# Two background jobs for the Strassen operands, and the mixers' weight remainders on VectorE and GpSimd in turn

## The chip, the cores and the metric

The kernel runs on one core of one Trainium2 chip. The metric is the device time of one execution in microseconds (us). The engines work side by side, each through its own queue in program order: TensorE (PE in the profile; PEld is its weight load), VectorE (DVE), ScalarE (ACT), GpSimd (POOL) and SyncE (SP, which starts most of the weight loads). Semaphores hold an instruction until the tile that it needs is written.

## The reference

One sequence of 512 tokens, width 1024, float32, goes through three layers. Each layer adds a mixer and then a SwiGLU FFN to the residual, both behind an RMS norm:

```
h = h + mix(rmsnorm(h))
h = h + (silu(u @ w_gate) * (u @ w_up)) @ w_down        # u = rmsnorm(h), d_ff = 2816
layer 0: mix = HGRN2, a gated linear recurrence, 8 heads of 128, chunks of 64 with decay
layer 1: mix = dilated causal attention, 12 heads in three groups
layer 2: mix = merge of NSA attention (compressed, selected, window) and GLA (4 heads, decay)
```

A final norm stands behind layer 1 and behind layer 2.

## The kernel before, in words

**Products.** Activations lie as eight tiles `x[k]` of 128 features by 512 tokens. A float32 operand is held as two tiles in TensorE's reduced format: a head `hi` (a rounded copy) and a remainder `lo` (the value minus its head). Each product is three matmuls, hi by hi, lo by hi and hi by lo (`mm3`). Nearly every instruction is recorded through one helper (line 250), so the tile names tell the operations apart: `u` is the normed input of a projection or of an FFN's first part, `og` HGRN's gated output, `oan` NSA's output, `obh` and `obl` GLA's, `mr` the merged one, `h` the FFN's hidden tile.

**Weights.** A weight arrives in units of up to 1024 columns in `w_raw` (SP's queue). ScalarE copies the head into a tile `w`, and then a subtraction makes the remainder, `w<-w_raw,w` in the profile. The class `Weights` plans both by a fixed schedule, 0.68 us per tile of columns: the head 8.8 us and the remainder 7.5 us ahead of use. The last argument of `plain` says who makes the remainder: `"v"` VectorE, `"g"` GpSimd, or `"d"`, an accumulating DMA on GpSimd's queue (`w<-in_ffn`), which the first part of each FFN uses. Before, GpSimd makes every second remainder of HGRN's last 8 units and of block 2's last 20; VectorE makes the rest.

**FFN.** Of 22 hidden tiles the first 5 (`FC`) are made by plain products from `u`: `gemm` over 10 tiles, gate and up in turn, whose results VectorE takes from PSUM (`gs<-ps,r_bc`, `h<-ps,sg`). The others go by Strassen's scheme on 256-token halves. Its operands, tiles named `E`, come from `strassen_operands` (line 1580): for each pair of x tiles two scaled copies (`E<-x,vec,r_bc`), four sums (`E<-E`), and for each of four operands a head on ScalarE and a remainder on VectorE (`E<-E,E`, or `E_3110<-E,E_3110` in the order lists). The routine is a generator: wherever it yields, it may be left until the tile that it names is ready. `ffn` starts it as a background job as soon as the norm's factor `r_bc` exists, runs the 10 plain tiles, then calls `drain`, which records whatever is left of the background jobs, and then the Strassen products, whose first chain of matmuls runs over all four pairs.

**The order.** Instructions are recorded in one pass. A planner (`Clock`) keeps an estimated time for every engine from fixed costs per operation (an n-column VectorE operation 0.08 + 0.00104 n us, GpSimd 0.13 + 0.0023 n us). After each tile of a projection `tick` goes through the background jobs and lets the first one that is due by this estimate take one step. So the decay steps of HGRN and GLA, the attention heads and the Strassen operands are laid between the projections' matmuls, and a change in an estimate, or in the number of jobs, moves instructions on all engines.

**Names in the mixers.** In HGRN and GLA the decay steps multiply Q and K (`GQ`, `GK` in GLA) by factors `T` or `GF`, `Sd` are masked scores, `cst,K` is a transpose of K, and `cst,o` sums the squares of a pair of heads' outputs `o` for the norm behind which `og` is made. In NSA `P` are probabilities, `PT` their transposes, `VV` the values, `ks` rotated keys.

Of the kernel before, what the change touches and what calls it, by code (L numbers as in the profile page):

```python
# [17 lines left out]
KD = 8  # L18
FF = 22
# [44 lines left out]
FC = 5  # L64

SHARED = {"hgrn": 8, "blk2": 20}

# [113 lines left out]
class Clock:  # L185
# [3 lines left out]
    def __init__(self, hop):  # L189
        self.hop = hop  # L190
        self.free = {"pe": 0.0, "v": 0.0, "a": 0.0, "g": 0.0}
        self.written, self.read = {}, {}
        self.held = []
# [68 lines left out]
class Weights:  # L262
# [7 lines left out]
    def __init__(self, prog, ctx, aps):  # L270
        tc = prog.tc
        self.nc, self.v, self.a, self.g = tc.nc, prog.v, prog.a, prog.g
        self.pool = ctx.enter_context(tc.tile_pool(name="w", bufs=self.ROOM))
        self.units, self.loads, self.todo, self.live = [], [], [], 0
        now = 0.0
        for sec, segments in weight_plan():
            off = 0
            for kind, body in segments:
                if kind == "c":
                    first = sec.startswith("ffn") and off == 0  # L280
                    units = plan_units(sec, body)
                    for n, (cur, w) in enumerate(units):
                        ap = aps[sec][off:off + 128 * w].rearrange("(p n) -> p n", p=128)
                        off += 128 * w
                        widths = [len(c[2]) for c in cur]
                        shared = n >= len(units) - SHARED.get(sec, 0)
                        self.plain(ap, widths, w, now, "d" if first else "g" if shared and n % 2 else "v")
                        now += w / 128 * self.TILE
                    continue
                order = strassen_order(len(body))  # L290
                groups = []
                for _, pairs, _, _ in body:
                    n = 128 * len(pairs)
                    aps_g = []
                    for w in (2 * n, n, n):
                        aps_g.append(aps[sec][off:off + 128 * w].rearrange("(p n) -> p n", p=128))
                        off += 128 * w
                    groups.append({"n": n, "aps": aps_g, "tiles": {}, "split": {}})
                for i, (g, p) in enumerate(order):
                    groups[g].setdefault("at", {})[p] = now + self.SLOT * i  # L300
                    self.units.append(("s", groups[g], p))
                for grp in groups:
                    self.group(grp, grp is groups[-1])
                now += self.SLOT * len(order)
        self.todo.sort(key=lambda x: x[0])
        self.n_todo = self.n_load = 0
        self.at, self.pos, self.idx, self.now = 0, 0, 0, 0.0
        self.look = 1
# [159 lines left out]
class Program:  # L468
# [1108 lines left out]
        self.residual_gemm(merged, "ffn2")  # L1577


    def strassen_operands(self, gain, X):  # L1580

        v, a = self.v, self.a
        for k in range(0, KD, 2):
            B1, B2, t13, t24 = [self.s2("E", (128, 2, 256)) for _ in range(4)]
            for B, i in ((B1, k), (B2, k + 1)):
                v.scalar_tensor_tensor(
                    B.rearrange("p a n -> p (a n)"), self.x[i], gain[:, i:i + 1], self.r_bc, op0=ALU.mult, op1=ALU.mult)
            yield [B2]
            v.tensor_sub(t13[:, 0], B1[:, 0], B1[:, 1])
            v.tensor_sub(t13[:, 1], B2[:, 1], B1[:, 1])  # L1590
            ops, Y = [], {}
            for src, names in ((B1[:, 0:1], ("a1",)), (B2, ("c", "b2")), (t13, ("b1", "a3")), (t24, ("a2", "a4"))):
                if src is t13:
                    yield [t13]
                    v.scalar_tensor_tensor(t24[:, 0], t13[:, 0], -1.0, B2[:, 1], op0=ALU.mult, op1=ALU.subtract)
                    v.scalar_tensor_tensor(t24[:, 1], t24[:, 0], -1.0, B2[:, 0], op0=ALU.mult, op1=ALU.subtract)
                if src is t24:
                    yield [t24]
                P = self.s2("E1", (128, 2, 1, 256), F32R) if len(names) == 1 else self.s4("E2", (128, 2, 2, 256), F32R)
                a.copy(P[:, 0], src)  # L1600
                ops.append((P, src))
                Y.update({p: (P[:, 0, i], P[:, 1, i]) for i, p in enumerate(names)})
            for P, src in ops:
                yield [P]
                v.tensor_sub(P[:, 1], src, P[:, 0].bitcast(F32))
            X.append(Y)

    def strassen(self, X, afters):

# [15 lines left out]
    def ffn(self, inner, gain_name, pre=None, gain=None, operands=True, residues=False):  # L1625
        v, a, g = self.v, self.a, self.g
        n1, n2 = slice(0, 256), slice(256, 512)
        hh, sr, X, late = [None] * FF, {}, [], []

        def splits():  # L1630
            n, h = late.pop(0)
            hh[n] = self.split(h, "h")

        def evac_up(i, ps):
            if i % 2 == 0:
                gs, sg = self.s2("gs"), self.s2("sg")
                v.tensor_mul(gs, ps, self.r_bc)
                a.activation(sg, gs, AF.Silu)
                g.tensor_mul(sg, sg, self.r_bc)
                sr[i // 2] = sg  # L1640
            else:
                h = self.s2("h")
                v.tensor_mul(h, ps, sr.pop(i // 2))
                late.append((i // 2, h))
            while late and (i % 2 == 0 or len(late) > 1):
                splits()

        self.after_norm = lambda: self.spawn(self.strassen_operands(self.V[inner], X), [self.r_bc])
        self.gemm(self.u, 2 * FC, evac_up, lead=2, hooks_at=(4, 6))
        self.drain()  # L1650
        self.u = None

        def up(i):

            gt, f = self.s2("G"), self.s2("h")

            def c(ps):
                v.tensor_add(gt[:, n1], gt[:, n1], ps)
                a.activation(gt[:, n1], gt[:, n1], AF.Silu)

            def b2(ps):
                while late:
                    splits()
                v.tensor_add(gt[:, n2], gt[:, n2], ps)
                a.activation(gt[:, n2], gt[:, n2], AF.Silu)

            def a3(ps):
                v.tensor_add(f[:, n2], f[:, n2], ps)
                v.scalar_tensor_tensor(f[:, n2], f[:, n2], -1.0, gt[:, n2], op0=ALU.mult, op1=ALU.mult)

            def a4(ps):
                v.scalar_tensor_tensor(f[:, n1], ps, -1.0, gt[:, n1], op0=ALU.mult, op1=ALU.mult)
                hh[i] = self.split(f, "h")

            return {
                "a1": lambda ps: a.copy(gt[:, n1], ps), "b1": lambda ps: a.copy(f[:, n2], ps),
                "a2": lambda ps: a.copy(gt[:, n2], ps), "b2": b2, "c": c, "a3": a3, "a4": a4,
            }

        def lazy(i):  # L1680

            made = {}

            def step(p):
                def go(ps):
                    if not made:
                        made.update(up(i))
                    made[p](ps)
                return go

            return {p: step(p) for p in S_AT}

        for half in range(2):
            mine = slice(FH * half, FH * half + FH)
            self.strassen(X, [lazy(i) for i in range(FH * half if half else FC, FH * half + FH)])
            if half == 1:
                X.clear()
                self.norm_begin(self.V[gain_name] if gain_name else gain, pre=pre, operands=operands, residues=residues)

            def evac_dn(m, ps):  # L1700
                if not operands and m == KD - 2:
                    a.activation(self.sm("warm", (128, 1)), self.eps, AF.Sqrt)
                v.tensor_add(self.x[m], self.x[m], ps)
                if half == 1:
                    self.norm_feed(m)

            last = half == 1 and not operands
            self.gemm(hh[mine], 7 if last else 8, evac_dn, lead=2)
            if not last:
                hh[mine] = [None] * FH  # L1710
        if last:
            self.finish(hh[mine])
        else:
            self.hooks.extend([self.norm_stats, self.norm_bc])
# [207 lines left out]
```

## Time and profile before

| | us |
|---|---|
| median of 3 runs | 2176.64 (2174.81 to 2180.24) |
| profiled execution | 2178.28 |
| its span in the trace | 2176.5 |

The profiled execution is what the rows below show; 1.8 us lie outside its span. In a timeline row stand the start in us, the busy time, engine, line, operation, out<-in, shapes, the count of joined instructions and, in brackets, how long the engine had idled and which engine's tile ended that. PEclk is the granted clock of TensorE as a share of the full 2.4 GHz.

### The profile page before, as it was taken

The numbers are of one execution on the slowest core, as the hardware profiler recorded it, in microseconds if no ns is written. First come the engines' busy times: TensorE is split into PE (matmuls) and PEld (weight loads), VectorE is DVE, ScalarE is ACT, GpSimd is POOL, SyncE is SP. The second block draws the span as 40 slices with busy tenths as digits, with TensorE's granted clock in tenths as the row PEclk, the third lists the DMA queues.
The fourth block names the chain that finished last, engine by engine and source line by source line (L and its number), as shares of the span: only waits on it lengthen the run. The fifth ranks groups of instructions, "written<-read, shape, count | busy, mean of one in ns | idle before, by whom it ended". The sixth has DMA issues, their size and how long they took to land.

```text
span 2176.5 us, 30591 instructions
## 1 busy us (share of the span) xinstructions
PE 2095.2 (96%) x11819; PEld 1841.8 (85%) x11819; DVE 1346.6 (62%) x2444; ACT 1030.6 (47%) x1819; POOL 375.5 (17%) x352
## 2 busy tenths in 40 slices
PE   9999889999999999999899999989999899899998
PEld 7888777989988998888888998978787688888997
DVE  5779736736755556554754765567776554755762
ACT  5343345625643343445543644244554636544653
POOL 2211222101101112112100104021301143100101
PEclk9999989999999999999999999999999899999999
DMA  6212336534642222227453763221121127453651
GB/s 216 78 49 61 106 83 137 135 124 112 152 148 97 89 77 77 78 78 169 106 156 75 155 173 121 90 81 39 60 68 59 39 76 175 102 155 80 155 168 39
DMA packets 80513, 230.66 MB, mean 106 GB/s; under 512 B 8992, under 2 KB 11056, under 8 KB 80368
## 3 DMA queue, kind: packets, MB, share of 16 engines
q1 hardware_dynamic: 60928, 183.86, 26.2%
q0 software_dynamic: 18288, 42.75, 11.8%
q8 instruction: 93, 1.52, 0.3%
q10 hardware_dynamic: 1152, 2.10, 0.3%
q14 instruction: 52, 0.43, 0.1%
HBM read 226.57 MB, written 2.10 MB: 105 GB/s over the span
## 4 chain that ended last, share of the span: by engine, by line
PE 74%; DVE 12%; ACT 6%; issue 4%; DMA 2%; POOL 1%; SPq 0%; DVEq 0%; ACTq 0%; POOLq 0%
PE ps L250 74%; DVE w L250 3%; ACT w L250 3%; DMA w_raw<-in_ffn 2%; DVE Sd L250 1%; DVE w_raw L250 1%; DVE Q L250 1%; DVE E L250 1%; DVE P L250 1%; ACT h L250 1%; DVE h L250 0%; ACT L250 0%; DVE K L250 0%; DMA w_raw<-in_hgrn 0%; DVE G L250 0%
## 5 line engine op out<-in xcount | busy, mean ns | idle before, releaser
L250 PE MATMUL ps<-u,w 128*128 128x512 f32 x2640 | 658.5, 400 | 4.0 <-DVE w L250 2.6
L250 DVE TENSOR_TENSOR w<-w_raw,w 128x1024 fp32r<-128x1024 f32 (+2 forms) x365 | 422.7, 1162 | 251.5 <-ACT w L250 197.8
L250 PEld LDWEIGHTS ps<-u,w 128*128 128x128 f32 x2640 | 486.8, 189 | 105.3 <-issue 6.5
L250 PE MATMUL ps<-E,w 128*128 128x256 f32 x4284 | 525.0, 285 | 28.5 <-DVE E L250 11.8
L250 PEld LDWEIGHTS ps<-E,w 128*128 128x128 f32 x4284 | 520.9, 193 | 32.9 <-DVE E L250 12.4
L250 ACT CAST w<-w_raw 128x1024 fp32r<-128x1024 f32 (+2 forms) x499 | 444.2, 903 | 200.9 <-DVE w L250 126.9
L250 PE MATMUL ps<-h,w 128*128 128x512 f32 (+1 forms) x1617 | 361.3, 385 | 0.5 <-DVE x L250 0.5
L250 PEld LDWEIGHTS ps<-h,w 128*128 128x128 f32 x1617 | 299.0, 188 | 60.9 <-DVE x L250 0.7
L343 POOL DMA_DIRECT2D w<-in_ffn x120 | 104.1, 868 | 675.6 <-ACT w L250 438.1
L250 PE MATMUL ps<-w,u 128*128 128x512 f32 (+1 forms) x672 | 153.8, 385 | 2.7 <-DVE u L250 2.6
L250 DVE TENSOR_TENSOR x<-x,ps 128x512 f32<-128x512 f32 (+1 forms) x73 | 49.5, 679 | 163.4 <-PE ps L250 163.4
L250 PEld LDWEIGHTS ps<-w,u 128*128 128x128 f32 x672 | 134.1, 223 | 15.2 <-DVE u L250 3.1
L250 DVE TENSOR_TENSOR w_raw<-w_raw 128x512 f32<-128x512 f32 x204 | 132.9, 686 | 9.7 <-DMA w_raw<-in_ffn 8.0
L250 ACT ACTIVATE P<-P,nm 128x128 f32<-128x128 f32 (+2 forms) x112 | 55.2, 494 | 141.8 <-DVE nm L250 131.0
L250 POOL TENSOR_TENSOR sq_acc<-sq_acc,sq 128x512 f32<-128x512 f32 x48 | 63.7, 1332 | 321.4 <-ACT sq L250 321.3
L250 ACT CAST h<-h 128x512 fp32r<-128x512 f32 x66 | 40.7, 617 | 118.4 <-DVE h L250 118.4
L250 ACT ACTIVATE w<-w 128x512 fp32r<-128x512 f32 (+1 forms) x120 | 88.5, 737 | 3.0
L250 DVE TENSOR_TENSOR h<-h 128x512 fp32r<-128x512 f32 x66 | 54.0, 819 | 53.4 <-ACT h L250 53.4
L250 ACT ACT_TABLE_LOAD x49 | 62.9, 1283 | 34.9 <-PE ps L250 11.4
L250 ACT ACTIVATE u<-x,vec 128x512 fp32r<-128x512 f32 x40 | 28.9, 722 | 94.1 <-DVE x L250 92.1
L250 POOL TENSOR_TENSOR t<-t,t 128x512 f32<-128x512 f32 x24 | 40.7, 1697 | 175.7 <-DVE t L250 175.7
L250 PE MATMUL ps<-ao,w 128*128 128x512 f32 x288 | 68.0, 393 | 1.3 <-ACT ao L250 1.3
(295 smaller groups left out, 2191.5 us busy)
## 6 DMA issues: line engine op xcount, KB each, us to landing
w_raw<-in_ffn SPq DMA_DIRECT2D x147, 512.0 KB, 3.6
w_raw<-in_ffn SPq DMA_DIRECT2D x102, 256.0 KB, 3.3
w_raw<-in_attn SPq DMA_DIRECT2D x48, 512.0 KB, 3.5
w_raw<-in_blk SPq DMA_DIRECT2D x47, 512.0 KB, 3.5
w<-in_ffn POOLq DMA_DIRECT2D x90, 256.0 KB, 4.2
w_raw<-in_hgrn SPq DMA_DIRECT2D x36, 512.0 KB, 3.6
w<-in_ffn POOLq DMA_DIRECT2D x30, 512.0 KB, 5.7
w_raw<-in_blk SPq DMA_DIRECT2D x7, 404.0 KB, 3.2
```

What stands on the lines that cost most here:

```text
L250: r = f(*args, **kw)
L343: self.nc.gpsimd.dma_start(lo, ap, accum_op=ALU.add)
```

## The change

`REST = "vg"` takes the place of `SHARED`: in every mixer (HGRN, attention, block 2) even units' remainders are made by VectorE and odd ones' by GpSimd; the FFNs' stay on VectorE. And `strassen_operands` is started twice, once for the pairs k = 0 and 4, once for k = 2 and 6; the list `X` of operand sets is made beforehand, and each job fills its own entries.

```diff
-SHARED = {"hgrn": 8, "blk2": 20}
+REST = "vg"
...
-                        shared = n >= len(units) - SHARED.get(sec, 0)
-                        self.plain(ap, widths, w, now, "d" if first else "g" if shared and n % 2 else "v")
+                        self.plain(ap, widths, w, now, "d" if first else "v" if sec.startswith("ffn") else REST[n % 2])
...
-    def strassen_operands(self, gain, X):
+    def strassen_operands(self, gain, X, mine):
...
-        for k in range(0, KD, 2):
+        for k in mine:
...
-            ops, Y = [], {}
+            ops, Y = [], X[k // 2]
...
-            X.append(Y)
...
-        hh, sr, X, late = [None] * FF, {}, [], []
+        hh, sr, X, late = [None] * FF, {}, [{} for _ in range(KD // 2)], []
...
-        self.after_norm = lambda: self.spawn(self.strassen_operands(self.V[inner], X), [self.r_bc])
+        def strassen_operands():
+            for n in range(2):
+                self.spawn(self.strassen_operands(self.V[inner], X, range(2 * n, KD, 4)), [self.r_bc])
+
+        self.after_norm = strassen_operands
```

Counted in the order of both programs, 60 remainders go from VectorE to GpSimd: 18 in HGRN (4 of them 512 wide), 24 in attention, 18 in block 2. GpSimd makes 74 in place of 14. SP's order is the same in both.

On VectorE, the end of the first FFN's plain part reads so before; `E_3110` to `E_3118` are the last pair's operands, `h<-ps,sg` takes the last plain tile from PSUM:

```order
L250 SCALAR_TENSOR_TENSOR E<-x,vec,r_bc 128x512 x2
L250 TENSOR_TENSOR w<-w_raw,w 128x512
L250 TENSOR_TENSOR w_raw<-w_raw 128x512 x2
L250 TENSOR_TENSOR h<-ps,sg 128x512
L250 TENSOR_TENSOR E<-E 128x256 x2
L250 SCALAR_TENSOR_TENSOR E<-E 128x256 x2
L250 TENSOR_TENSOR E_3110<-E,E_3110 128x256
L250 TENSOR_TENSOR E_3112<-E,E_3112 128x512
L250 TENSOR_TENSOR E_3116<-E,E_3116 128x512
L250 TENSOR_TENSOR E_3118<-E,E_3118 128x512
```

At the same place of the changed program `gs<-ps,r_bc` takes the ninth of the ten plain tiles:

```order
L249 TENSOR_TENSOR h<-ps,sg 128x512
L249 TENSOR_TENSOR w_raw<-w_raw 128x512 x2
L249 TENSOR_TENSOR E_2966<-E,E_2966 128x256
L249 TENSOR_TENSOR w_raw<-w_raw 128x512 x2
L249 TENSOR_TENSOR E_2968<-E,E_2968 128x512
L249 TENSOR_TENSOR E_3011<-E,E_3011 128x512
L249 TENSOR_TENSOR E_3044<-E,E_3044 128x512
L249 TENSOR_TENSOR gs<-ps,r_bc 128x512
L249 TENSOR_TENSOR h<-h 128x512
L249 TENSOR_TENSOR w<-w_raw,w 128x1024 x2
```

All operands stand ahead of the ninth tile's `gs` instead of behind the tenth tile's `h`; the other two FFNs read the same.

On TensorE, the end of HGRN, where the out-projection `og,w` begins, before:

```order
L250 MATMUL ps<-og,w 128x512 x3
L250 MATMUL ps<-V,Sd 128x128 x2
L250 MATMUL ps<-St,Q 128x128
L250 MATMUL ps<-V,Sd 128x128
L250 MATMUL ps<-St,Q 128x128
L250 MATMUL ps<-V,Sd 128x128
L250 MATMUL ps<-St,Q 128x128
L250 MATMUL ps<-og,w 128x512 x3
L250 MATMUL ps<-cst,o 128x128 x8
L250 MATMUL ps<-og,w 128x512 x120
```

And in the changed program, where `u,w` is still the in-projection:

```order
L249 MATMUL ps<-V,Sd 128x128
L249 MATMUL ps<-St,Q 128x128
L249 MATMUL ps<-V,Sd 128x128
L249 MATMUL ps<-St,Q 128x128
L249 MATMUL ps<-u,w 128x512 x18
L249 MATMUL ps<-cst,o 128x128 x8
L249 MATMUL ps<-u,w 128x512 x3
L249 MATMUL ps<-og,w 128x512 x192
```

The last heads' decay matmuls and norm sums have left the out-projection, whose 192 matmuls now stand in one piece. The same goes for NSA's last heads: before, six pieces of other work stand within its out-projection `oan,w`, and in the changed program its 96 matmuls are unbroken.

On VectorE, two steps of GLA's decay in block 2 before (each ends in a masked `Sd`):

```order
L250 TENSOR_TENSOR GK<-GK,GF 128x256
L250 COPY_PREDICATED Sd<-lvl,ps 128x512
L250 TENSOR_TENSOR w<-w_raw,w 128x1024
L250 TENSOR_TENSOR ks<-rot,ks 64x512 x4
L250 SCALAR_TENSOR_TENSOR qraw<-ps,r_bc 128x512
L250 TENSOR_TENSOR GQ<-GQ,GF 64x256 x2
L250 TENSOR_TENSOR GK<-GK,GF 128x256
```

And in the changed program:

```order
L249 TENSOR_TENSOR GK<-GK,GF 128x256
L249 COPY_PREDICATED Sd<-lvl,ps 128x512
L249 TENSOR_TENSOR GQ<-GQ,GF 64x256 x2
L249 TENSOR_TENSOR GK<-GK,GF 128x256
L249 COPY_PREDICATED Sd<-lvl,ps 128x512
```

The remainder, the keys `ks` and `qraw` no longer stand between the two steps.

## Rows read from the trace of the kernel before

**Rows 1.** The page: span, then busy time, share and instructions of each engine.
```profile
span 2176.5 us, 30591 instructions
PE 2095.2 (96%) x11819; PEld 1841.8 (85%) x11819; DVE 1346.6 (62%) x2444; ACT 1030.6 (47%) x1819; POOL 375.5 (17%) x352
```

**Rows 2.** Timeline of PE where the first FFN's Strassen products begin.
```profile
379.87 0.50 PE L250 MATMUL ps<-E,w 128*128 128x256 f32 x2 [2.38 <-ACT E L250]
384.30 3.90 PE L250 MATMUL ps<-E,w 128*128 128x256 f32 x20 [3.93 <-DVE E L250]
```

**Rows 3.** Timeline of DVE at the same place.
```profile
378.64 1.40 DVE L250 SCALAR_TENSOR_TENSOR E<-x,vec,r_bc 128x512 f32<-128x512 f32 x2
...
382.37 0.74 DVE L250 TENSOR_TENSOR E<-E 128x256 f32<-128x256 f32 x2
...
383.83 2.22 DVE L250 TENSOR_TENSOR E<-E,E 128x256 fp32r<-128x256 f32 x4
```

**Rows 4.** Windows: stretch, length, engines' busy time, PEclk, DMA; sum of three at PEclk 0.50.
```profile
320.00:376.00 56.00, 55.25 (x247) 45.77 (x248) 31.53 (x52) 31.42 (x44) 14.22 (x14) 1.00 0.71 155
...
sum 20.40, PE 10.66 PEld 10.59 DVE 18.74 ACT 6.64 POOL 0.00; mean PE 3.55 PEld 3.53 DVE 6.25 ACT 2.21 POOL 0.00
```

**Rows 5.** Timeline of PE at the end of HGRN.
```profile
268.62 0.88 PE L250 MATMUL ps<-cst,K 128*128 128x128 f32 x3 [6.62 <-DVE K L250]
285.76 1.97 PE L250 MATMUL ps<-cst,o 128*128 128x128 f32 x8 [3.17 <-DVE o L250]
289.13 11.19 PE L250 MATMUL ps<-og,w 128*128 128x512 f32 x36 [1.39 <-ACT og L250]
```

**Rows 6.** Windows of HGRN; the sum is over 264.3:274.5 and 284.7:294.9, PEclk 0.50.
```profile
180.00:195.00 15.00, 15.00 (x83) 12.85 (x82) 14.45 (x41) 6.99 (x10) 2.73 (x3) 1.00 0.24 73
...
sum 20.40, PE 13.63 PEld 11.12 DVE 8.21 ACT 5.68 POOL 4.87; mean PE 6.81 PEld 5.56 DVE 4.10 ACT 2.84 POOL 2.44
```

**Rows 7.** Groups of DVE and POOL: count, busy us, mean ns of one, idle before.
```profile
L250 DVE TENSOR_TENSOR w<-w_raw,w 128x1024 fp32r<-128x1024 f32 x286 | 365.4, 1280 | 218.8 <-ACT w L250 168.8 <-PE ps L250 45.6 <-issue 3.7
L250 POOL TENSOR_TENSOR w<-w_raw,w 128x1024 fp32r<-128x1024 f32 x13 | 31.4, 2417 | 84.5 <-ACT w L250 59.8 <-DVE nsum L250 17.3 <-DVE w L250 7.4
L250 DVE TENSOR_TENSOR K<-K,T 128x256 f32<-128x256 f32 x5 | 2.1, 417 | 0.0
```

**Rows 8.** Timeline of POOL and DVE beside a remainder, in HGRN and in NSA.
```profile
265.69 2.50 POOL L250 TENSOR_TENSOR w<-w_raw,w 128x1024 fp32r<-128x1024 f32 x1 [7.42 <-DVE w L250]
265.91 2.56 DVE L250 TENSOR_TENSOR K<-K,T 128x256 f32<-128x256 f32 x1
...
1714.51 2.08 DVE L250 TENSOR_TENSOR mg<-ps,mg 128x512 f32<-128x512 f32 x3
1715.05 2.37 POOL L250 TENSOR_TENSOR w<-w_raw,w 128x1024 fp32r<-128x1024 f32 x1 [9.99 <-ACT w L250]
```

**Rows 9.** Timeline of block 2: DVE before a GLA step, then PE's waits.
```profile
1458.29 2.88 DVE L250 TENSOR_TENSOR ks<-rot,ks 64x512 fp32r<-64x512 f32 x4
1463.26 2.05 PE L250 MATMUL ps<-GQ,GK 128*128 128x128 f32 x8 [5.37 <-DVE GK L250]
1539.02 0.98 PE L250 MATMUL ps<-u,w 128*128 128x512 f32 x3 [1.54 <-DVE w L250]
```

**Rows 10.** Timeline of PE at the end of NSA.
```profile
1716.43 1.22 PE L250 MATMUL ps<-oan,w 128*128 128x512 f32 x2 [3.54 <-ACT oan L250]
1731.73 2.91 PE L250 MATMUL ps<-PT,VV 128*128 128x512 f32 x8 [2.84 <-ACT PT L250]
1742.73 5.49 PE L250 MATMUL ps<-oan,w 128*128 128x512 f32 x17 [3.38 <-ACT oan L250]
```

**Rows 11.** Windows of NSA's end; sum over 1714.9:1721.7, 1732:1738.8, 1742.2:1745.6, PEclk 0.50.
```profile
sum 17.00, PE 14.09 PEld 11.48 DVE 11.90 ACT 6.25 POOL 2.75; mean PE 4.70 PEld 3.83 DVE 3.97 ACT 2.08 POOL 0.92
```

**Rows 12.** Window of attention, then the start of the first FFN on PE.
```profile
705.00:915.00 210.00, 209.97 (x990) 184.11 (x988) 127.59 (x346) 78.99 (x171) 38.15 (x22) 1.00 0.25 81
...
320.75 5.51 PE L250 MATMUL ps<-u,w 128*128 128x512 f32 x23 [1.39 <-DMA w<-in_ffn]
```

## The prediction

> **What bounds the kernel now.** I read the page first: TensorE is busy 2095.2 of 2176.5 us, VectorE 1346.6, GpSimd 375.5 [rows 1]. Work of TensorE is neither added nor removed, so the change can gain only what TensorE idles, and what it loses while its clock is low. I therefore went along TensorE's timeline for every wait over half a microsecond, then to the engine that each names, and took the granted clock behind it from the windows. Three places hold most of them, and each shows the 2.4 GHz clock falling to 1.2 GHz (PEclk 0.50) after the wait.
>
> First, each FFN's Strassen part begins with two waits, 2.38 and 3.93 us [rows 2]; the same two figures stand at 1050 and 1864 us, so three times 6.31 = 18.9 us. The reader is to see that the last pair's operands are being made just then: VectorE's scaled copies end at 380.0, the sums begin at 382.37, the remainders at 383.83 [rows 3]. Before it, from 320 to 376, VectorE was busy 31.53 of 56 us [rows 4]: the operands are late because one job takes the pairs one by one, not for want of VectorE's time. In the 6.8 us behind each of these second waits (380.3, 1052.7 and 1865.1 on) the clock is at 0.50; the 10.66 us of matmuls there [rows 4] would take half at full clock, another 5.3 us.
>
> Second, the end of HGRN waits 6.62, 3.17 and 1.39 us for VectorE's K and o and ScalarE's og [rows 5], and 13.63 us of matmuls run at half clock [rows 6]: 11.2 + 6.8 = 18 us at most. Third, block 2: 5.37 us for GK, 1.54 for a remainder [rows 9], and at the end of NSA 3.54, 2.84 and 3.38 us [rows 10], with 14.09 us of matmuls at half clock [rows 11].
>
> **Part 1, two jobs.** No operation is added. With one job, `tick` can serve only the one pair that it stands at, and each yield waits for another engine; with two, one pair's heads pass ScalarE while the other's sums pass VectorE. The order shows all operands ahead of the ninth plain tile's gs, so both waits should go: 18.9 us, and with them the half clock, 5.3. What moves forward is VectorE work of 1.40 + 0.74 + 2.22 us in [rows 3], with two further sums, taken like the first two, 5.1; the 24 us that VectorE idles between 320 and 376 hide it. Without that cover the 5 us would delay gs and h of the plain tiles, and then the remainders of the first Strassen weights. I take **−24** (bounds: −18.9 if the clock falls for another reason, −24.2).
>
> **Part 2, remainders on GpSimd.** Each full-width one takes 1.28 us off VectorE's queue and puts 2.42 on GpSimd's [rows 7]. With 60 more GpSimd is at some 375 + 60 x 2.42 = 520 of 2176 us, so it is no bound. But the moved work isn't free for VectorE. K<-K,T, 0.42 us alone [rows 7], took 2.56 when it began just after GpSimd's remainder at 265.69, and ended with it at 268.4 us, while the three mg beside another remainder, which read PSUM, took 2.08, 0.69 each [rows 8]. So the price on VectorE lies between 0 (it idles, or reads PSUM) and 2.14 us for each remainder. By mean I take half of GpSimd's 2.42, 1.2, as an operation that comes somewhere within it would: the relief is then 1.28 − 1.2, nearly nothing where VectorE is dense.
>
> The Trainium skill, "SBUF — State Buffer", section "Who interferes with whom", says that VectorE's second port pair is GpSimd's only one, under an exclusive lock. This speaks against the change; the trace agrees with 2.56 in place of 0.42. By that rule every remainder could cost a two-input operation up to the whole 2.42, and the balance would be a loss, to some 2194; that is the rival of the other sign below.
>
> In *HGRN* VectorE is busy up to 14.45 of 15 us [rows 6], so 18 moved remainders relieve it by 18 x 0.08, about 1.4 us, and not by 18 x 1.28. What helps is the order: the last decay matmuls and norm sums have left the out-projection, and 18 matmuls of in-projection stand ahead of the last cst,o, about 18 x 5.51 / 23 = 4.3 us [rows 12] against the 3.17 us waited there. Against it stands that the planner counts a whole remainder as saved, so that VectorE may trail the order. Bounds: 0 and −18; I take less than half, **−8**.
>
> In *GLA* the 5.37 us wait stands behind a remainder, four ks of 2.88 us and qraw on VectorE [rows 9]; in the new order none of them is between the two steps. That is nearly the whole wait: **−5** (bounds −2, if ks delays another step, and −5.4). The wait of 1.54 us for a remainder [rows 9]: **−1** (bounds 0 and −1.5).
>
> At the *end of NSA* the waits are 9.8 us and half of 14.09 is 7.0, 16.8 in all [rows 10, 11]. The new order has the last heads' work ahead of the out-projection, whose 96 matmuls are unbroken; but the softmax chain of the last head must end before it, and something of the wait can stand ahead of the first instead. Bounds 0 and −17: **−7**.
>
> In *attention* TensorE is busy 209.97 of 210 us [rows 12]: nothing to gain. The 24 remainders there cost nothing as long as VectorE's idle 82 us hide the blocks; without that cover each would cost up to 2.14.
>
> **New waits.** A remainder on GpSimd comes 1.1 us later than on VectorE, and any GpSimd operation ahead of it adds its own. Behind it on GpSimd's queue stand the squares of the norm and the accumulating DMAs for the next FFN; the first FFN already waits 1.39 us for one [rows 12]. A remainder more ahead of it would make that 3.8; at three FFNs, and for a few late remainders in HGRN, I take **+4** (bounds 0, and +12 for 3 x 2.42 and four remainders late by 1.1).
>
> **The sum** against the profiled 2178.28: −24 − 8 − 5 − 1 − 7 + 4 = −41, 2137.3. The median of the runs is 1.6 lower than the profiled one, so I give 2136.
>
> **The rivals.**
> *Mixers neutral*: the relief of 0.08 us each is no relief, GLA's and NSA's gains are paid back as waits for late remainders and a trailing VectorE. Then only part 1 is left: 2176.6 − 24 = 2153. For it speaks VectorE's density in HGRN; against it that GLA's wait is plainly made by what the new order moves away.
> *All of it gone*: the mixers' whole 18 + 5.4 + 1.5 + 16.8 = 42 go with the 24, and no wait is new: 2176.6 − 66 = 2111. The unbroken out-projections speak for it; the last heads' chains, which must run somewhere, against.
> *FFN gain given back*: the earlier operands push gs and h, so that the plain tiles' PSUM is late, or the first Strassen weights are: half of part 1, −12, with the mixers as forecast, −17: 2148. VectorE's idle 24 us speak against.
> *The jobs don't do what they say*: a job is served only when the planner finds it due; if heads on ScalarE lag behind the estimate, TensorE waits for E as before, and the mixers alone give −17: 2160. The order, which leaves at least one plain tile's matmuls between, speaks against.
> *Slower, the blocked VectorE*: each of the 36 remainders in HGRN and block 2 meets a two-input operation, as at 265.91, which costs 2.14 − 1.28 = 0.86 net, and TensorE waits for all of it: +31, with part 1's −24 +7, 2184; at the whole 2.42 each, 1.14 x 36 = +41, 2194. It decides from a loss of 24 + 6.5 = 30 us in the mixers on. Half of these operations read PSUM or come when GpSimd rests, and TensorE waits for VectorE only at some of them; that is against it.
>
> **How the numbers follow.** Forecast 0.50, mixers neutral 0.24, all gone 0.13, FFN gain given back 0.04, jobs without effect 0.04, slower 0.05. The likeliest gives the time, 2136. Its own range, with half of its bounds on each side, is 2120 to 2147. The range for 8 in 10 takes in mixers neutral and both small cases, and leaves out most of "all gone" and the slower one: 2112 to 2162. What a measurement here can tell from no change is about 0.3%, 6.5 us, so 2170 and 2183 are the limits: faster 0.50 + 0.24 + 0.13 + 0.04, less 0.02 for their tails, and half of the jobs' case, 0.91; slower 0.05; same 0.04, from the tails and the other half.
>
> **What would show it.** Part 1 is right if the Strassen parts begin without a wait for E and at full clock, and VectorE's last E remainder ends before the last plain tile. Part 2: w on GpSimd 74 times at about 2.4 us; K, Q and w of VectorE lengthened beside them by 1 to 1.2 us each on average; TensorE's wait for GK at GLA's first steps gone; the out-projections of HGRN and NSA free of waits over 3 us. The prediction is wrong if TensorE shows new waits for POOL's w in the mixers, if VectorE's o and K come as late as before against the new order, or if each FFN's first plain tile waits several us for the accumulating DMA.

## The result and the profile after

The changed kernel takes 2149.4 us (2146.56 to 2150.93, 4 runs) against 2177.85 (2174.81 to 2180.24, 4 runs) of the kernel before beside it: 0.9869 of the time, 95% interval 0.9851 to 0.9886, some 28.5 us less. The forecast was 2136, range 2112 to 2162; the time lies nearest to the case "mixers neutral", 2153.

The page of the changed kernel, the span and the engines' busy time; [rows 1] answer to it:

```profile
span 2148.8 us, 30642 instructions
PE 2088.1 (97%) x11819; PEld 1830.8 (85%) x11819; DVE 1322.3 (62%) x2384; ACT 1028.7 (48%) x1819; POOL 515.2 (24%) x412
```

GpSimd has 139.7 us more, close to 60 x 2.42 = 145. VectorE has only 24.3 less, where 60 remainders were some 73 (1.28 each [rows 7], a few of them shorter).

Where did the 27.7 us of span come from? I cut both traces at the first matmul of each part (its tile names change there), and did the same for every kernel run later. Each figure is from one profiled execution, in us; the third column adds the three Strassen parts that begin an FFN, the fourth the three second Strassen halves. The other parts differ by less than 2 us.

| kernel | HGRN | Strassen, first | Strassen, second | attention | block 2 to `mr,w` | span |
|---|---|---|---|---|---|---|
| before | 320.7 | 211.3 | 341.2 | 312.3 | 409.9 | 2176.5 |
| changed | 321.5 | 185.5 | 346.8 | 313.2 | 400.6 | 2148.8 |
| changed, again | 321.2 | 186.0 | 341.4 | 313.2 | 402.2 | 2146.7 |
| e1 two jobs only | 318.6 | 185.4 | 338.4 | 312.3 | 411.6 | 2147.0 |
| e2 remainders only | 320.7 | 212.2 | 337.4 | 313.2 | 400.0 | 2164.6 |
| e5 full remainders, not read | 320.7 | 185.4 | 337.2 | 313.2 | 402.1 | 2141.0 |
| e4 cut remainders, not read | 309.6 | 186.0 | 339.3 | 312.7 | 390.8 | 2119.2 |
| e10 cut, filler on VectorE | 316.4 | 185.9 | 339.3 | 312.6 | 396.1 | 2131.1 |
| e12 cut, transfers on GpSimd | 312.4 | 186.1 | 340.9 | 312.5 | 391.7 | 2124.1 |
| e3 block 2 on GpSimd | 323.1 | 185.6 | 338.6 | 312.3 | 402.1 | 2144.3 |
| e13 the same, none in HGRN | 317.3 | 184.8 | 342.4 | 312.3 | 400.5 | 2140.1 |
| e11 block 2 GpSimd, HGRN DMA | 321.1 | 184.9 | 337.8 | 312.3 | 402.1 | 2139.2 |
| e8 HGRN and block 2 DMA | 317.7 | 186.0 | 340.3 | 312.3 | 408.9 | 2146.8 |
| e9 planner counts the block | 318.8 | 185.8 | 338.7 | 315.1 | 407.3 | 2146.3 |

From before to the changed kernel: −25.8 in the three Strassen starts, −9.3 in block 2, +0.8 in HGRN, +0.9 in attention, +5.6 in the second Strassen halves; the parts not shown add 0.1, so the sum is −27.7.

The timeline of TensorE in the changed kernel where the first FFN's Strassen products begin, and the window of the plain tiles ahead of it (columns as in [rows 4]):

```profile
376.98 3.03 PE L249 MATMUL ps<-E,w 128*128 128x256 f32 x24
```

```profile
320.00:376.00 56.00, 54.53 (x244) 45.14 (x245) 37.52 (x64) 34.66 (x49) 14.24 (x14) 1.00 0.72 157
```

The row has no bracket: both waits of [rows 2] are gone, the granted clock stays at 1.00 behind it, and VectorE took 6.0 us more into the idle time ahead (31.53 before), where 5.1 were forecast. The other two FFNs begin without these waits too, and at 1.00.

In HGRN the reader is to see one block, that is, an operation of VectorE held up by a remainder of GpSimd. Three rows of the changed kernel, VectorE, GpSimd and TensorE, and the window behind them:

```profile
178.63 2.89 DVE L249 TENSOR_TENSOR Q<-Q,T 128x256 f32<-128x256 f32 x2
178.47 2.45 POOL L249 TENSOR_TENSOR w<-w_raw,w 128x1024 fp32r<-128x1024 f32 x1 [0.81 <-ACT w L249]
181.57 1.65 PE L249 MATMUL ps<-Q,K 128*128 128x192 f32 x4 [3.09 <-DVE Q L249]
...
180.50:187.30 6.80, 5.73 (x16) 5.05 (x17) 6.49 (x18) 0.00 (x0) 0.41 (x1) 0.50 0.00 0
```

The first Q began at 178.63, 0.16 us behind GpSimd's remainder, and lasted until 0.3 us after that had ended at 180.9. TensorE waited 3.09 us for the pair of them, and its clock fell to 0.50 for 6.8 us from 180.5 on. The rows of K in [rows 8] are of the same kind.

GLA and the end of NSA in the changed kernel, which answer to [rows 9, 10]:

```profile
1441.56 2.45 DVE L249 TENSOR_TENSOR GK<-GK,GF 128x256 f32<-128x256 f32 x1
1441.20 2.52 POOL L249 TENSOR_TENSOR w<-w_raw,w 128x1024 fp32r<-128x1024 f32 x1
1444.15 2.04 PE L249 MATMUL ps<-GQ,GK 128*128 128x128 f32 x8 [3.01 <-DVE GK L249]
...
1527.97 2.33 PE L249 MATMUL ps<-u,w 128*128 128x512 f32 x9 [1.46 <-DVE w L249]
...
1715.80 0.73 PE L249 MATMUL ps<-oan,w 128*128 128x512 f32 x2 [1.39 <-ACT oan L249]
```

The wait of 5.37 us for GK has become one of 3.01, because GpSimd's remainder now falls on GK itself. The wait of 1.54 us for a remainder of VectorE is still there, with 1.46. NSA's end went as the order said: of 3.54, 2.84 and 3.38 us waits of 1.39 and 0.43 are left, and the clock is at 1.00. In between, two waits over 2 us are new:

```profile
1514.54 0.63 PE L249 MATMUL ps<-cst,Pc 128*64 128x128 f32 x4 [2.29 <-DVE Pc L249]
...
1539.95 1.11 PE L249 MATMUL ps<-ks,qs 128*128 128x256 f32 x4 [3.50 <-ACT oa L249]
```

The first is again a VectorE operation, 2.55 us beside a remainder; the second, for ScalarE's oa, is 3.50 in the cut-remainder kernel too, so it belongs to the new order.

### The profile page after: what moved, and what is told of

The parts are those of the page before. It is cut to its first block, busy times and chain, and to the rows that moved or that the text cites. A ratio compares the mean times of both kernels' runs of the same rounds, so it can differ in the third digit from the quotient of the medians.

```text
span 2148.8 us, 30642 instructions
## 1 busy us (share of the span) xinstructions
PE 2088.1 (97%) x11819; PEld 1830.8 (85%) x11819; DVE 1322.3 (62%) x2384; ACT 1028.7 (48%) x1819; POOL 515.2 (24%) x412
## 4 chain that ended last, share of the span: by engine, by line
PE 69%; DVE 14%; ACT 7%; DMA 4%; issue 4%; POOL 1%; SPq 0%; DVEq 0%; POOLq 0%; ACTq 0%
PE ps L249 69%; ACT w L249 4%; DMA w_raw<-in_ffn 4%; DVE w L249 3%; DVE w_raw L249 2%; DVE Q L249 2%; DVE Sd L249 2%; ACT h L249 1%; DVE h L249 1%; ACT G L249 1%; DVE P L249 1%; DVE G L249 1%; DMA w_raw<-in_hgrn 0%; ACT L249 0%; DVE ks L249 0%
## 5 line engine op out<-in xcount | busy, mean ns | idle before, releaser
L249 PE MATMUL ps<-u,w 128*128 128x512 f32 x2640 | 666.3, 402 | 3.8 <-DVE w L249 1.8
L249 PE MATMUL ps<-E,w 128*128 128x256 f32 x4284 | 519.4, 283 | 14.1 <-ACT G L249 8.2
L249 DVE TENSOR_TENSOR w<-w_raw,w 128x1024 fp32r<-128x1024 f32 (+2 forms) x305 | 354.8, 1166 | 212.8 <-ACT w L249 155.5
L249 POOL TENSOR_TENSOR w<-w_raw,w 128x1024 fp32r<-128x1024 f32 (+3 forms) x74 | 176.5, 2385 | 374.9 <-ACT w L249 310.2
```

What stands on the lines that cost most here:

```text
L249: r = f(*args, **kw)
```

## The experiments

After the result stood, the theory was this. **A**: the jobs give the 25.6 us of the Strassen starts by themselves; in the mixers, GpSimd's remainders hold VectorE's operations up, which takes back what the move relieved. Its rivals: the new order keeps the waits whatever VectorE's operations take; GpSimd's remainders come too late for TensorE; GpSimd's other work comes later; or the planner, which knows nothing of the block, lays work too early.

**e1, two jobs only.**

```diff
-REST = "vg"
+SHARED = {"hgrn": 8, "blk2": 20}
...
+                        shared = n >= len(units) - SHARED.get(sec, 0)
+                        self.plain(ap, widths, w, now, "d" if first else "g" if shared and n % 2 else "v")
```

> Two operand jobs side by side, the remainders shared between VectorE and GpSimd as before the change. Theory A (the jobs are worth what stands at the three Strassen starts, 7.0 + 9.3 + 9.3 = 25.6 us by the two traces, and do not need the remainders): 2177.9 - 25 = 2153 us, no wait for E at the three starts. Rival B (the operands come early only because remainders have also left VectorE, or the jobs cost something elsewhere): 2160 us or more, with a wait for E left at a start.

Measured 2148.0 us, ratio 0.9873 (0.9859 to 0.9886). The Strassen starts are as short as in the whole change (185.4 against 185.5), without a wait for E over 0.3 us. The jobs alone are worth as much as the whole change; A's 2153 was 5 us too slow, for the other parts of this run were short too (HGRN 318.6, second halves 338.4).

**e2, remainders only.** One job as before; against the kernel before:

```diff
-SHARED = {"hgrn": 8, "blk2": 20}
+REST = "vg"
...
-                        shared = n >= len(units) - SHARED.get(sec, 0)
-                        self.plain(ap, widths, w, now, "d" if first else "g" if shared and n % 2 else "v")
+                        self.plain(ap, widths, w, now, "d" if first else "v" if sec.startswith("ffn") else REST[n % 2])
```

> One operand job as before, the mixers' remainders on VectorE and GpSimd in turn. Theory A (block 2 gains 9 us, HGRN and attention lose about 1 each): 2177.9 - 7 = 2171 us, with the waits of 2.38 and 3.93 us still at the three Strassen starts. Rival B (the remainders do nothing by themselves, block 2's gain was a matter of the run): 2178 us.

Measured 2167.2 us, ratio 0.9960 (0.9948 to 0.9973): 8.4 us less. The waits are where they were, here the first two:

```profile
379.82 0.51 PE L250 MATMUL ps<-E,w 128*128 128x256 f32 x2 [2.37 <-ACT E L250]
384.26 5.99 PE L250 MATMUL ps<-E,w 128*128 128x256 f32 x34 [3.93 <-DVE E L250]
```

The remainders gain 9.9 us in block 2 (400.0), nothing in HGRN (320.7). Yet beside the two jobs they add nothing that can be measured (0.9869 and 0.9873).

**e5 and e4, the remainders without their readers, whole and cut.** Both keep the changed kernel's instructions and order on each engine; `SWAP` gives TensorE the head in place of GpSimd's remainders. In e4 (the last lines) the remainder itself shrinks to 32 columns as well, and the planner is told the full cost.

```diff
+        if unit["rest"] == "g":
+            SWAP[id(r[1])] = r[1], r[0]
...
-            r = f(*args, **kw)
+            r = f(*[SWAP.get(id(x), (x, x))[1] for x in args], **kw)
...
+                if rest == "g":
+                    raw = unit["raw"][:, :w]
+                    self.nc.gpsimd.tensor_sub(lo[:, :32], raw[:, :32], hi[:, :32].bitcast(F32))
+                    self.g.clock.issue("g", "tensor_sub", [lo], [raw, hi])
```

> As the kernel without the long remainders, but GpSimd makes the full remainders and TensorE still reads the head in their place: VectorE is lengthened as in the changed kernel, and no matmul waits for a remainder of GpSimd. Theory A (lateness of GpSimd's remainders costs little, the lengthening of VectorE costs the rest): 2149.4 - 2 = 2147 us. Rival B (TensorE waits for late remainders of GpSimd): as fast as the kernel with cut remainders, 2134 to 2140 us.

> The changed kernel in the same order on every engine, but GpSimd's 74 remainders are cut to 32 columns and TensorE reads the head in their place (the second of the three matmuls of those units uses a wrong operand, so that the time alone counts). Theory A (VectorE gives back through operations lengthened beside GpSimd's remainders what it was relieved of, 16 of 20 us in HGRN, and this is why the mixers gained so little): HGRN's first 321 us shorten by 8 to 12 us, block 2 by 4 to 8, whole 2149.4 - 15 = 2134 us. Rival B (the new order is what keeps the waits, whatever VectorE's operations take): within 4 us of 2149.

Measured: e5 2146.2 us, ratio 0.9862 (0.9849 to 0.9876); e4 2122.2 us, ratio 0.9753 (0.9740 to 0.9766), on one chip. So late remainders cost nothing that can be told (e5 against 2149.4 and 2147.5 of the change), and the length of 74 operations of GpSimd costs 24 us, with the order on every engine unchanged. That is more than the 15 us that A gave e4. The three rows of the block in HGRN above, in e4 (VectorE, GpSimd, TensorE):

```profile
172.72 0.80 DVE L250 TENSOR_TENSOR Q<-Q,T 128x256 f32<-128x256 f32 x2
172.56 0.35 POOL L331 TENSOR_TENSOR w<-w_raw,w 128x32 fp32r<-128x32 f32 x1 [0.81 <-ACT w L250]
173.57 0.92 PE L250 MATMUL ps<-Q,K 128*128 128x192 f32 x4 [1.00 <-DVE Q L250]
```

The same two operations take 0.80 us in place of 2.89, and TensorE's wait is 1.00 in place of 3.09: 2.09 us each, one for one, and the fall of the clock behind it is gone. The windows of HGRN and block 2, of e5 and then of e4, add that up:

```profile
0.00:320.70 320.70, 300.83 (x1525) 251.21 (x1525) 216.09 (x424) 140.96 (x264) 115.92 (x97) 0.99 0.29 97
1334.10:1736.20 402.10, 380.58 (x1959) 317.40 (x1959) 260.37 (x555) 187.42 (x378) 117.52 (x88) 0.98 0.20 69
```

```profile
0.00:309.60 309.60, 297.94 (x1524) 250.13 (x1524) 200.14 (x423) 139.88 (x262) 71.60 (x97) 1.00 0.30 100
1322.10:1712.90 390.80, 376.38 (x1960) 314.63 (x1959) 245.79 (x557) 187.91 (x380) 68.23 (x85) 0.99 0.21 71
```

VectorE's busy time, the third figure behind the comma, falls by 16.0 and 14.6 us for the same operations. In these windows 22 and 23 remainders were cut (those that GpSimd made before the change too, and not only the moved ones), so each had held VectorE for 0.73 and 0.63 us on average, 0.68 over both. The two parts are 11.1 and 11.3 us shorter; A had given block 2 only 4 to 8. In attention the same is worth 0.5: TensorE's one wait over 0.5 us there, 1.28 for ao, stands in the kernel before too.

**e10, a filler on VectorE.** As e4, with a VectorE subtraction of 5/8 of the columns behind each cut remainder, to give VectorE the lost time back as plain work.

```diff
+                    self.nc.vector.tensor_sub(lo[:, 32:32 + w * 5 // 8], raw[:, 32:32 + w * 5 // 8], hi[:, 32:32 + w * 5 // 8].bitcast(F32))
```

> The kernel with GpSimd's remainders cut to 32 columns and the head read in their place, with one VectorE subtraction of 5/8 of the remainder's columns (some 0.8 us at full width, a result that nothing reads) added behind each: about the 16.0 + 12.5 us in 36 that VectorE is lengthened by in HGRN and block 2 when the remainders are whole. Theory A (the 24 us are VectorE's lost time): most of them come back, 2140 to 2148 us. Rival B (they come from GpSimd, whose other work is done sooner when its remainders are short): as without the filler, 2122 us.

Measured 2132.4 us, ratio 0.9810 (0.9796 to 0.9825). Window of HGRN:

```profile
0.00:316.40 316.40, 298.43 (x1524) 249.81 (x1524) 216.02 (x446) 140.81 (x263) 75.89 (x97) 1.00 0.29 98
```

VectorE is as busy as in e5 (216.02 against 216.09; in block 2 262.38 against 260.37), but only 6.8 of the 11.1 us came back, and 5.3 of 11.3 in block 2. That lies between the theories: VectorE's time is about half of it (12.1 of 22.4 us in the traces, 10.2 of 24.0 in the medians), not all.

The order of TensorE's matmuls is the same in e5, e4 and e10, so its waits can be compared matmul by matmul. In the two parts e4 has 14.1 us of them less than e5, and the filler brings 7.9 of these back. What it doesn't bring back stands at the blocks shown above: the waits for Q, GK and Pc, 3.09, 3.00 and 2.31 us in e5, are 0.99, 1.46 and 0 in e10, 5.9 us less:

```profile
177.14 0.92 PE L250 MATMUL ps<-Q,K 128*128 128x192 f32 x4 [0.99 <-DVE Q L250]
...
1433.10 1.15 PE L250 MATMUL ps<-GQ,GK 128*128 128x128 f32 x8 [1.46 <-DVE GK L250]
```

Most of the other 8.3 us between e5 and e4 is TensorE's own busy time (300.83 against 297.94 us, 380.58 against 376.38) at a granted clock of 0.99 and 0.98 in place of 1.00 and 0.99.

**e12, GpSimd kept busy by transfers.** As e4, with two small transfers issued on GpSimd behind each cut remainder.

```diff
+                    for i in (1, 2):
+                        self.nc.gpsimd.dma_start(lo[:, 32 * i:32 * i + 32], ap[:, :32])
```

> The kernel with GpSimd's remainders cut to 32 columns and the head read in their place, and behind each two transfers of 32 columns (which nothing reads) issued on GpSimd's queue: some 0.9 us of GpSimd each by the issues of the FFNs, so that GpSimd is taken for about as long as by a whole remainder (0.35 + 1.8 against 2.4 us) without touching VectorE's operations. Theory A (the 24 us come from operations of VectorE that last until GpSimd's remainder ends): as without the transfers, 2122 to 2126 us. Rival B (what the filler left open, 14 us, is GpSimd's other work that comes later): 2132 us or more.

Measured 2125.9 us, ratio 0.9774 (0.9760 to 0.9789), A's figure. But such an issue took 0.56 us, not 0.9, so that GpSimd got back only half of its time (95.09 us in HGRN; 71.60 in e4, 115.92 in e5):

```profile
0.00:312.40 312.40, 297.81 (x1525) 249.32 (x1525) 203.26 (x423) 140.46 (x262) 95.09 (x141) 1.00 0.34 102
```

HGRN and block 2 lost 2.8 and 0.9 us. They needn't be GpSimd's delay alone: VectorE too is 3.1 us busier in HGRN than in e4 (203.26 against 200.14), since two u and a Q last about 1 us longer each, beside other operations of GpSimd that now come later. If the 3.7 us were all GpSimd's own delay, and twice the time cost twice as much, it would be about 7 of the 22.4 us of both parts. How large it is stays open; the waits at the three blocks and TensorE's busy time account for most of what the filler left without it.

**e6, the change once more**, with no edit.

> The changed kernel once more, beside three others on one chip, to tell what of its FFNs' second Strassen halves (113.9, 115.2 and 117.7 us in its trace, 112.3 to 113.0 in three of the kernels run since) belongs to that run alone. Theory A (late weight transfers of that one run): 112 to 113.5 us each, whole 2145 us. Rival B (the change delays those transfers): again 117 in the last FFN and 2149 us.

Measured 2147.5 us, ratio 0.9872 (0.9856 to 0.9889). The second halves are 113.9, 113.6 and 113.9 us: the 117.7 of the first trace did not come again, but with 341.4 they are above e5's 337.2, whose order is the same. Over all fourteen traces they lie between 337.2 and 346.8, so a difference of some us in that column says nothing about an edit. The time of 2147.5 lies between the two theories, and neither is shown.

**e3 and e13, remainders on GpSimd in block 2 alone**, with HGRN's last four on GpSimd as before, or with none (`SHARED = {"blk2": 1000}`).

```diff
-REST = "vg"
+SHARED = {"hgrn": 8, "blk2": 1000}
```

> Two operand jobs, every second remainder of block 2 on GpSimd, HGRN and attention as before the change. Theory A (the remainders gain in block 2 alone, some 10 us, and cost 3 in HGRN and 1 in attention): 2148.0 - 8 = 2140 us. Rival B (block 2's gain comes back elsewhere or depends on the run): 2148 us, as the two jobs alone.

> Two operand jobs, every second remainder on GpSimd in block 2 alone, none in HGRN and attention. Theory A (in HGRN a remainder on GpSimd gives VectorE back as much as it takes): HGRN 319 to 323 us and the whole 2142 us, as with HGRN's last four on GpSimd. Rival B (HGRN's last four, one of which blocks K, cost the waits at its end): HGRN 315 us, the whole 2136 us.

Measured 2142.3 us (ratio 0.9857, 0.9842 to 0.9871) and 2142.2 us (0.9853, 0.9836 to 0.9869). Both are faster than the change by some 0.1 to 0.2%, less than the intervals can tell apart. HGRN took 323.1 us in e3, and 318.6 and 320.7 in e1 and in the kernel before, which share its remainders alike; the change's 321.5 lies within that spread and e13's 317.3, without any on GpSimd, 1.3 us below it. So whether HGRN's last four cost anything isn't shown; the 2142 of A came, the 2136 of B didn't.

**e8 and e11, remainders by ScalarE and an accumulating DMA** (e8: HGRN from unit 10 on, counted from 0, and block 2; e11: HGRN alone in this way, block 2 on GpSimd).

```diff
-REST = "vg"
+REST = "vd"
...
-"v" if sec.startswith("ffn") else REST[n % 2])
+"v" if sec.startswith("ffn") or sec == "attn" or sec == "hgrn" and n < 10 else REST[n % 2])
```

> Two operand jobs; the odd units' remainders of HGRN (from the tenth unit on) and of block 2 are made by ScalarE's negated copy and an accumulating DMA on GpSimd's queue, as the FFNs' first part does, attention's all by VectorE. Theory A (it was the block on VectorE that cost 11 us in HGRN and 11 in block 2, and a DMA blocks nothing): VectorE is relieved without a price, ScalarE has half of its time free: 2148 - 18 = 2130 us. Rival B (ScalarE's extra copies, about 1 us each, delay the chains that it is part of, and the DMA comes late): 2145 us or more.

> Two operand jobs; HGRN's odd remainders from the tenth unit on by ScalarE and an accumulating DMA (317.7 us for HGRN in the kernel that had it), block 2's on GpSimd (400.0 to 402.2 us), attention's on VectorE. If stages add up: 2142.3 less some 3 to 5, 2138 us. If HGRN's 317.7 was a matter of the run (318.6 to 323.1 with the old sharing): 2142 us.

Measured 2148.8 us (ratio 0.9885, 0.9870 to 0.9899) and 2140.9 us (0.9855, 0.9838 to 0.9871). My 2130 for e8 was wrong. Windows of HGRN and block 2 in e8, and two of its waits:

```profile
0.00:317.70 317.70, 299.41 (x1524) 250.56 (x1525) 200.20 (x427) 154.65 (x277) 76.23 (x92) 0.99 0.46 127
1332.00:1741.00 409.00, 384.30 (x1960) 319.38 (x1959) 248.11 (x556) 214.31 (x405) 82.92 (x86) 0.97 0.37 97
```

```profile
1549.08 3.35 PE L249 MATMUL ps<-u,w 128*128 128x512 f32 x7 [3.00 <-DMA w<-in_blk]
...
1706.31 1.22 PE L249 MATMUL ps<-oan,w 128*128 128x512 f32 x2 [4.69 <-ACT oan L249]
```

VectorE has the 200.20 us of e4, but ScalarE 154.65 in place of 139.88 in HGRN and 214.31 in place of 187.91 in block 2, and TensorE waits for ScalarE and for the transfers. Here VectorE's relief didn't buy the time, since another engine of the same chains paid for it. HGRN's order is the same in e8 and e11, and took 317.7 and 321.1 us: the 317.7 was a matter of the run. e11, 2140.9, is the lowest of the kernels that compute all of it, and not told apart from e3 and e13.

**e9, a planner that counts the block.**

```diff
+        if eng == "g":
+            self.free["v"] += 0.4 * self.cost(eng, op, outs[0], ins)
```

> The changed kernel with a planner that adds 0.4 of each GpSimd operation's time to its estimate of VectorE. Theory A (VectorE's time itself is missing, not the estimate of it): within 4 us of the changed kernel, 2145 to 2151 us. Rival B (TensorE waits because the planner lays the decay steps too early for a VectorE that trails): HGRN and block 2 shorten by 5 us or more together, 2141 us.

Measured 2150.8 us, ratio 0.9892 (0.9877 to 0.9907): HGRN 2.7 us shorter than in the change, block 2 6.7 longer. With this estimate of VectorE's load the time doesn't come back; another share than 0.4 was not tried.

## Why the prediction was right, and where it was off

**Part 1, −24.** Right: the three starts give −25.8 (1.6 beyond the bound of −24.2, and from where isn't shown), the waits and the half clock of [rows 2, 4] are gone, VectorE's idle time took the moved 6.0 us, and e1 shows that this half needs nothing of the other. The jobs alone carry the change.

**Part 2, the price on VectorE.** The step was right in kind: [rows 8] gave bounds of 0 and 2.14 us, I took 1.2, and e5 against e4 gives 0.68 for each remainder in HGRN and block 2 (the 36 in e10's expectation leave out the remainders that GpSimd made before). From 1.2 I concluded that the relief in HGRN is next to nothing, 1.4 us; the windows show 219.74 to 215.58, 4.2.

**HGRN, −8.** This is the step that failed, as I put it: "What helps is the order." The old waits at its end, 11.2 us, did go with the order. But TensorE then waited for Q, K and o earlier on, 3.09 us at the Q above and 0.5 to 1.8 us at ten other places, and HGRN stayed at 321.5 us. I had priced the blocks by VectorE's mean load, and let the order's gain stand beside it; a block on an operation that TensorE waits for can pass on in full, as at this Q. Without the blocks the same order is 11.1 us shorter than the kernel before (e4), but there VectorE and GpSimd are relieved as well; with plain work of VectorE in the blocks' place it is 4.3 us shorter (e10). So GpSimd's whole remainders took the gain back, and what the order is worth by itself isn't shown.

**Block 2, −5 − 1 − 7 = −13.** −9.3 came, in part by luck, for terms missed on both sides. NSA's end gave more than 7: its waits fell from 9.8 to 1.8 us, and the clock no longer fell there. GLA's term was too large, since the remainder that left the queue came back as a block on GK (5.37 to 3.01 us). The −1 didn't come, for that wait is still 1.46 us. And I had no term for Pc's 2.29 us, a block as well, and oa's 3.50, which comes with the new order.

**Attention, 0.** +0.9 in the kernels with GpSimd's whole remainders there, and +2.8 in e9, whose planner laid them otherwise.

**New waits, +4.** Late remainders cost nothing that can be told (e5 against the change), and each FFN's first part takes as long as before, or 1.6 us more in the first FFN in some runs. The +5.6 of the first trace stands elsewhere, in the second Strassen halves, where it varies from run to run.

**The sum.** −41 forecast, −28.5 measured, −27.7 in the traces. Of the 13.3 us missing there 8.8 are HGRN's, 3.7 block 2's, 0.9 attention's and 1.7 come from the second Strassen halves and the parts not shown (+5.7 against the +4 of new waits), while the three starts gave 1.8 more. "Mixers neutral" came nearest in time, though not as I described it: late remainders cost nothing that can be told, the mixers gave −7.6 us, and the second halves of that run took 5.6 back. The range of the likeliest case was added wrong: half of the bounds that I named is 12.6 us below and 16.1 above, so 2123 to 2152 and not 2120 to 2147. What stays open is why the 9 us that block 2 gains with GpSimd's remainders (e2, e3, e13) leave no trace in the medians of the change against e1. The traces put it at +2.6 to 2.9 us in HGRN, 0.9 in attention, and the rest in the second Strassen halves and the first FFN's start, which vary by as much. Those 318.6 us of e1 are the lowest of three traces with HGRN in that order.

## What to carry to other kernels

Work that a background job does in sequence may be late for want of a second job, not of engine time: look for idle time of its engine ahead of the wait, as in [rows 4], and split the job. Moving a subtraction from VectorE to GpSimd saved VectorE 1.28 us here and held its other operations for 0.68 on average; mg, which read PSUM, was not held [rows 8]. Price such a move by a row in which both ran at once, and ask which operation it will hold, and not only how long one is held on average. Before judging what an engine's load costs, cut that one operation short in an unchanged order, give the time back to each engine in turn, and compare the waits instruction by instruction.

## What the runs showed of the hardware

Even the smallest operations of VectorE are held. In the changed kernel, around attention, VectorE's timeline of a sum of 128x4, of four scalings beside a remainder of GpSimd and of a remainder of its own, and then GpSimd's:

```profile
903.75 2.29 DVE L249 TENSOR_TENSOR rl<-rl,c 128x4 f32<-128x4 f32 x1
...
794.30 3.17 DVE L249 TENSOR_SCALAR P<-P,rl 128x128 f32<-128x128 f32 x4
...
667.24 2.33 DVE L249 TENSOR_TENSOR w<-w_raw,w 128x1024 fp32r<-128x1024 f32 x1
```

```profile
903.62 2.40 POOL L249 TENSOR_TENSOR w<-w_raw,w 128x1024 fp32r<-128x1024 f32 x1 [5.79 <-ACT w L249]
...
794.21 2.39 POOL L249 TENSOR_TENSOR w<-w_raw,w 128x1024 fp32r<-128x1024 f32 x1 [6.39 <-ACT w L249]
...
667.20 1.29 POOL L249 TENSOR_TENSOR sq_acc<-sq_acc,sq 128x512 f32<-128x512 f32 x1 [6.18 <-ACT sq L249]
668.45 3.37 POOL L249 TENSOR_TENSOR w<-w_raw,w 128x1024 fp32r<-128x1024 f32 x1
```

The sum of 128x4, 0.16 us at 794.10, took 2.29 at 903.75. Of the scalings, which read one tile and a column, the first lasted 2.38 us, until the remainder that had begun just before it ended, and the other three 0.34 each. And the block goes both ways: at 667.24 VectorE's remainder began while GpSimd's sum ran until 668.49, and ended at 669.57; GpSimd's next remainder, begun at 668.45, took 3.37 us in place of 2.42.

The Trainium skill, "SBUF — State Buffer", section "Who interferes with whom", says that it is the order of issue that decides which of the two engines waits, and that VectorE's scaling can take both ports of the pair. The rows at 667 and 794 agree with both.
